# Sliding windows of an image batch: a plain unit filled and stored ahead of the second half-batch tile, in three pairs

## The chip, the core and the metric

The kernel runs on one core of a Trainium2 chip. The metric is the device time of one execution in microseconds, lower is better. Three engines matter: VectorE (DVE) and ScalarE (ACT) copy data within the on-chip memory SBUF, and GpSimd (POOL) issues indirect DMAs, whose destination rows come from an index tile. SyncE (SP) issues a few plain DMAs. The DMAs of all queues are carried out by the same 16 DMA engines.

## What is computed

The input x is 16 images of 64 channels of 64 x 64 f32 (16.8 MB). The output holds each 8 x 8 window with stride 4, that is 15 x 15 windows for each image (62.9 MB). Nothing is calculated; data is only moved.

```python
for i in range(n_h):
    for j in range(n_w):
        h_start = i * stride
        w_start = j * stride
        result[:, i, j] = x[:, :, h_start:h_start + window_size, w_start:w_start + window_size].copy()
```

One output row `(b, i, j)` is 64 x 8 x 8 f32 = 16 KB and contiguous.

## The kernel before

**Layout.** The whole input lies in one tile `L` of 128 partitions: a partition holds one half of the channels (`ch`, 2), one image (`b`, 16) and one quarter of the rows (`hq`, 4). The images are split into two half-batches of 8 (`y`, NY = 2), so that 32 partitions (`QP`) hold one half-batch and one channel half. A quarter of 16 rows has four window rows or slots (`s`); slots 0, 1 and 2 lie inside the quarter, slot 3 needs four rows of the next.

**Loads.** Eight DMAs on the queues of ACT and SP (line 115) bring the first channels through the buffers `GG` as a staging area, from where lines 125 to 132 copy them into `L`. Six DMAs on SP and 16 on POOL (line 58, called in lines 117 to 123) load the other channels straight into `L`, the half-batch y = 0 first and y = 1 behind it. POOL's loads and POOL's stores use the same queue.

**Buffers.** `GG` is four buffers of 128 partitions x 16 KB, one output row for each partition. `tile_()` (line 190) hands them out in turn, so a tile can be filled only when the store of the tile four places earlier has finished. There are 31 tiles.

**Three kinds of tile.**
- `part(y, j)` (line 195): one half-batch, slots 0 and 1, window columns j and j+1. It reads only the partitions of half-batch y. It takes 8 copies of 32 x 2048 f32, three on ACT and five on DVE, and one indirect store of 128 rows.
- `unit(j, 0, ...)`, a plain unit (line 212): all 16 images, slots 0 and 1, column j. It reads both half-batches. In the three pairs around the change it takes 4 copies of 64 x 2048, two on ACT and two on DVE, and one store of 128 rows.
- `unit(j, 2)`, a cross unit: slots 2 and 3. ACT copies; DVE fills its share with stream shuffles, which also fetch the rows of the next quarter. One store, of which 16 rows are dropped by the bounds check (112 are written).

`fill` (line 155) writes the copies of a unit; `scatter` (line 143) issues the store on POOL. Stores have no order among themselves, since each writes rows of its own.

**Order.** The program order in the source is the order on each engine. Tiles 0 to 2 are `part(0, 0)`, `part(0, 2)`, `part(0, 4)` (line 227). Then come three pairs (line 231), tiles 3 to 8: `part(1, 0)` and the plain unit of column 6, `part(1, 2)` and column 7, `part(1, 4)` and column 8. Behind them rounds of three cross units and one plain unit (line 234), tiles 9 to 28, and at the end two small tiles of column 14, which SP stores (lines 243 to 253).

Of the kernel before, what the change touches and what calls it, by code (L numbers as in the profile page):

```python
# [10 lines left out]
def kernel(  # L11
# [131 lines left out]
    def scatter(g, ix, j, s):  # L143
        st = nc.gpsimd.indirect_dma_start(  # L144
            out=o_v,
            out_offset=bass.IndirectOffsetOnAxis(ap=ix[:, 0:1], axis=0),
            in_=g.rearrange("p c r w -> p (c r w)"),
            in_offset=None,
            element_offset=(s * NW + j) * CFREE,
            bounds_check=B * NWIN - 1,  # L150
            oob_is_err=False,
        )
        free(st)

    def fill(g, half, s, j, lo, n, copies):

        d = slice(half * HP + lo, half * HP + lo + n)
        cols = slice(j * ST, j * ST + WS)
        for ch in (half, 1 - half):
            f = slice(ch * HP + lo, ch * HP + lo + n)  # L160
            cs = slice(ch * CL, (ch + 1) * CL)
            copy = copies[ch != half]
            if s < NSLOT - 1:
                copy(out=g[d, cs, :, :], in_=L[f, :, s * ST : s * ST + WS, cols])  # L164
            else:
                copy(out=g[d, cs, 0:ST, :], in_=L[f, :, s * ST : RB, cols])
                nc.vector.stream_shuffle(out=g[d, cs, ST:WS, :], in_=L[f, :, 0:ST, cols], mask=nxt)  # L167

    act, dve = nc.scalar.copy, nc.vector.tensor_copy
# [20 lines left out]
    def tile_():  # L190
        nonlocal at
        at += 1
        return G[(at - 1) % NG]

    def part(y, j):
        g = tile_()
        order = [(d, ch) for ch in range(CH) for d in range(P // QP)]
        for n, (d, ch) in enumerate(order):
            s, dj = d // NY, d % NY
            cols = slice((j + dj) * ST, (j + dj) * ST + WS)  # L200
            f = (ch * NY + y) * QP
            tc.keep_in_program_order(
                (act if n % 3 == 0 else dve)(  # L203
                    out=g[d * QP : (d + 1) * QP, ch * CL : (ch + 1) * CL, :, :],
                    in_=L[f : f + QP, :, s * ST : s * ST + WS, cols],
                )
            )
        scatter(g, (idx_y0, idx_y1)[y], j, 0)
# [3 lines left out]
    def unit(j, s, copies=(shf, mix)):  # L212
        nonlocal crossed
        g = tile_()
        if s == 0:
            fill(g, 0, 0, j, 0, HP, (act, copies[0]))
            fill(g, 1, 1, j, 0, HP, (act, copies[1]))
            scatter(g, idx, j, s)
        else:

            turn = 1 - crossed % 2
            crossed += 1
            fill(g, turn, s, j, 0, HP, (act, act))
            fill(g, 1 - turn, s + 1, j, 0, HP, (shf, mix))
            scatter(g, (idx_hi, idx_lo)[turn], j, s)
# [3 lines left out]
    plain = [(j, 0) for j in range(2 * EARLY, NW - 1)]  # L229
    cross = [(j, 2) for j in range(NW)]  # L230
    for n in range(EARLY):
        part(1, 2 * n)
        unit(*plain.pop(0), (dve, dve))
    while plain:
        for w in cross[:3]:
            unit(*w)
# [52 lines left out]
```

## Time and profile before

| | |
|---|---|
| median of three runs | 186.99 us (186.84 to 187.19) |
| the profiled execution | 187.06 us, span 185.3 us |
| DMA queue 0 (POOL: loads and stores) | 65.55 MB, 84.8% of 16 engines' span |
| DMA queue 1 (SP) | 8.13 MB, 11.0% |
| DMA queue 10 (ACT) | 2.10 MB, 3.1% |
| HBM read and written | 16.78 MB and 62.91 MB |
| L203 DVE COPY 32x2048 (half-batch tiles) | 30 of 1219 ns |
| L203 ACT COPY 32x2048 | 18 of 1897 ns |
| L164 ACT COPY 64x2048 (units) | 46 of 1897 ns |
| L164 DVE COPY 64x2048 | 6 of 1222 ns |
| L167 DVE STREAM_SHUFFLE 64x1024 | 30 of 1281 ns |

The span is the stretch that the profiler sees; some 1.8 us lie around it. Of the page's views, the tenths row shows how busy an engine, or the mean of the 16 DMA engines, was in each of 40 slices of 4.6 us. The timeline lists instructions by start and duration, equal neighbours merged ("x5"), with the idle time ahead of them and what ended it in brackets. The busy time by stretch can show a DMA share a little above 1, since packets overlap at their edges.

### The profile page before, as it was taken

The numbers are of one execution on the slowest core, as the hardware profiler recorded it, in microseconds if no ns is written. First come the engines' busy times: TensorE is split into PE (matmuls) and PEld (weight loads), VectorE is DVE, ScalarE is ACT, GpSimd is POOL, SyncE is SP. The second block draws the span as 40 slices with busy tenths as digits, with TensorE's granted clock in tenths as the row PEclk, the third lists the DMA queues.
The fourth block names the chain that finished last, engine by engine and source line by source line (L and its number), as shares of the span: only waits on it lengthen the run. The fifth ranks groups of instructions, "written<-read, shape, count | busy, mean of one in ns | idle before, by whom it ended". The sixth has DMA issues, their size and how long they took to land.

```text
span 185.3 us, 597 instructions
## 1 busy us (share of the span) xinstructions
DVE 154.2 (83%) x213; ACT 150.7 (81%) x100; POOL 48.3 (26%) x50
## 2 busy tenths in 40 slices
DVE  5002998999999999799999999999999999999600
ACT  0002999999999999998899999998999999899600
POOL 7400652033308071422222222222222222222000
DMA  4999999999999999999999999999999999999995
GB/s 151 398 410 399 402 402 399 390 382 426 433 424 435 428 428 439 432 430 424 435 430 432 428 432 428 439 417 435 424 423 428 410 435 414 421 428 403 442 414 216
DMA packets 10980, 75.81 MB, mean 409 GB/s; under 512 B 3280, under 2 KB 3280, under 8 KB 7376
## 3 DMA queue, kind: packets, MB, share of 16 engines
q0 software_dynamic: 8656, 65.55, 84.8%
q1 hardware_dynamic: 1744, 8.13, 11.0%
q10 hardware_dynamic: 576, 2.10, 3.1%
q14 instruction: 4, 0.03, 0.0%
HBM read 16.78 MB, written 62.91 MB: 430 GB/s over the span
## 4 chain that ended last, share of the span: by engine, by line
ACT 28%; DVE 28%; DMA 27%; issue 8%; POOL 2%; ACTq 1%; DVEq 0%; PEldq 0%
DVE GG L174 17%; ACT GG L203 17%; DMA L<-in_x_dram 14%; DMA out_dram<-GG,idx 13%; DVE GG L167 11%; ACT GG L164 7%; ACT GG L251 3%; POOL L L58 2%; ACT GG L178 1%; ACTq L284 0%; ACTq L203 0%; POOL pi L69 0%; DVEq L174 0%; PEldq L284 0%; ACTq L164 0%
## 5 line engine op out<-in xcount | busy, mean ns | idle before, releaser
L164 ACT COPY GG<-L 64x2048 f32<-64x2048 f32 x46 | 87.3, 1897 | 5.1 <-DMA out_dram<-GG,idx 2.7
L174 DVE STREAM_SHUFFLE GG<-L 64x1024 f32<-64x1024 f32 (+4 forms) x39 | 53.0, 1359 | 1.3
L167 DVE STREAM_SHUFFLE GG<-L 64x1024 f32<-64x1024 f32 x30 | 38.4, 1281 | 0.0
L203 DVE COPY GG<-L 32x2048 f32<-32x2048 f32 x30 | 36.6, 1219 | 1.8 <-DMA L<-in_x_dram 0.8
L203 ACT COPY GG<-L 32x2048 f32<-32x2048 f32 x18 | 34.1, 1897 | 0.7 <-DMA L<-in_x_dram 0.3
L132 DVE COPY L<-GG 32x2048 f32<-32x2048 f32 x10 | 11.9, 1234 | 13.7 <-DMA GG<-in_x_dram 13.6
L144 POOL DMA_INDIRECT out_dram<-GG,idx_y x6 | 11.0, 1838 | 26.3 <-DVE GG L203 13.2
L58 POOL DMA_DIRECT2D L<-in_x_dram x16 | 12.8, 809 | 19.0 <-DMA L<-in_x_dram 18.5
L144 POOL DMA_INDIRECT out_dram<-GG,idx_lo x8 | 7.7, 961 | 30.8 <-DVE GG L167 23.2
L132 ACT ACT_TABLE_LOAD x1 | 1.3, 1283 | 17.2 <-DMA GG<-in_x_dram 17.2
L144 POOL DMA_INDIRECT out_dram<-GG,idx x8 | 9.7, 1217 | 17.4 <-DVE GG L174 6.8
L144 POOL DMA_INDIRECT out_dram<-GG,idx_hi x7 | 6.7, 961 | 26.6 <-DVE GG L167 22.9
L132 ACT COPY L<-GG 32x2048 f32<-32x2048 f32 x6 | 11.2, 1894 | 0.1
L178 ACT COPY GG<-L 64x256 f32<-64x256 f32 (+2 forms) x21 | 10.2, 484 | 0.5
L164 DVE COPY GG<-L 64x2048 f32<-64x2048 f32 x6 | 7.3, 1222 | 0.2
L251 DVE COPY GG<-L 32x1280 f32<-32x1280 f32 x8 | 6.5, 818 | 0.4 <-DMA out_dram<-GG,idx_hi 0.3
L251 ACT COPY GG<-L 32x768 f32<-32x768 f32 x8 | 6.6, 829 | 0.1
L174 DVE LOAD_MASK_SELECT GG<-L x39 | 0.4, 9 | 1.4 <-ACT GG L164 1.0
L72 DVE TENSOR_SCALAR tb<-pi 128x1 int32<-128x1 int32 x1 | 0.2, 154 | 1.0 <-POOL pi L69 1.0
L179 DVE COPY GG<-L 64x1280 f32<-64x1280 f32 x1 | 0.9, 877 | 0.0
L78 DVE TENSOR_TENSOR th<-tc,tq 128x1 int32<-128x1 int32 x2 | 0.3, 156 | 0.0
L75 DVE TENSOR_SCALAR th<-tc 128x1 int32<-128x1 int32 x2 | 0.3, 154 | 0.0
(21 smaller groups left out, 3.0 us busy)
## 6 DMA issues: line engine op xcount, KB each, us to landing
L<-in_x_dram POOLq DMA_DIRECT2D x10, 768.0 KB, 18.4
L<-in_x_dram SPq DMA_DIRECT2D x6, 640.0 KB
GG<-in_x_dram ACTq DMA_DIRECT2D x4, 512.0 KB, 14.4
GG<-in_x_dram SPq DMA_DIRECT2D x4, 512.0 KB, 14.8
out_dram<-GG SPq DMA_DIRECT2D x2, 1024.0 KB, 10.1
L<-in_x_dram POOLq DMA_DIRECT2D x6, 128.0 KB, 18.2
out_dram<-GG,idx POOLq DMA_INDIRECT x8, 12.4
out_dram<-GG,idx_lo POOLq DMA_INDIRECT x8, 10.3
```

Of the source, the lines that this page charges most:

```text
L58: eng.dma_start(out=L[p0 : p0 + QP - HQ + 1 : HQ, c0:c1, :, :], in_=x_v[ch, y, q, :, c0:c1, :])
L75: nc.vector.tensor_scalar(out=d[:, :], in0=a[:, :], scalar1=float(m), scalar2=None, op0=ALU.mult)
L78: nc.vector.tensor_tensor(out=d[:, :], in0=a[:, :], in1=b[:, :], op=op)
L132: tc.keep_in_program_order(copy(out=L[d, c : c + PC, :, :], in_=S[ch][f, c : c + PC]))
L144: st = nc.gpsimd.indirect_dma_start(out=o_v, out_offset=bass.IndirectOffsetOnAxis(ap=ix[:, 0:1], axis=0), in_=g.rearrange("p c r w -> p (c ...
L164: copy(out=g[d, cs, :, :], in_=L[f, :, s * ST : s * ST + WS, cols])
L167: nc.vector.stream_shuffle(out=g[d, cs, ST:WS, :], in_=L[f, :, 0:ST, cols], mask=nxt)
L174: nc.vector.stream_shuffle(out=out, in_=in_, mask=same)
L178: act(out=out[:, 0:k], in_=in_[:, 0:k])
L179: other(out=out[:, k:], in_=in_[:, k:])
L203: (act if n % 3 == 0 else dve)(out=g[d * QP : (d + 1) * QP, ch * CL : (ch + 1) * CL, :, :], in_=L[f : f + QP, :, s * ST : s * ST + WS, cols],)
L251: copy(out=g[d, ch * CL + c0 : ch * CL + c1, :, :], in_=L[f, c0:c1, s * ST : s * ST + WS, cols])
```

## The change

Within each of the three pairs of line 231 the two tiles change places.

```diff
     plain = [(j, 0) for j in range(2 * EARLY, NW - 1)]
     cross = [(j, 2) for j in range(NW)]
     for n in range(EARLY):
+        unit(*plain.pop(0), (dve, dve))
         part(1, 2 * n)
-        unit(*plain.pop(0), (dve, dve))
     while plain:
```

The buffers go round as before, so the plain units now get tiles 3, 5 and 7 (buffers 3, 1, 3) and the half-batch tiles 4, 6 and 8 (buffers 0, 2, 0). On ACT two copies of a unit now stand ahead of three of a half-batch tile in each pair, on DVE two ahead of five, and on POOL the store with `idx` ahead of that with `idx_y1`. The number and the shapes of all instructions are the same. PE's and SP's streams are the same.

## The prediction

> **What bounds the kernel now.** I read the page's shares first, then the busy time by stretch, then the timeline between 44 and 90 us, then the list of waits, and last the trace's records of single DMA packets. Tiles are numbered 0 to 30 in the order in which the code takes a buffer; tile n lies in buffer n mod 4, and store n is its store.
>
> ```profile
> DVE 154.2 (83%) x213; ACT 150.7 (81%) x100; POOL 48.3 (26%) x50
> DMA  4999999999999999999999999999999999999995
> GB/s 151 398 410 399 402 402 399 390 382 426 433 424 435 428 428 439 432 430 424 435 430 432 428 432 428 439 417 435 424 423 428 410 435 414 421 428 403 442 414 216
> ```
>
> Both copy engines are over 80% busy, which looks like a bound. But the DMA row stands at 9 in every slice but the first and the last. By stretch (DVE, ACT and POOL busy, clock, DMA share, GB/s):
>
> ```profile
> 47.00:60.00 13.00, 12.66 (x12) 12.83 (x8) 5.50 (x3) 1.00 1.01 430
> 60.00:76.00 16.00, 14.62 (x12) 15.80 (x9) 5.82 (x4) 1.00 1.01 433
> 76.00:90.00 14.00, 13.44 (x24) 12.66 (x10) 2.89 (x3) 1.00 1.00 429
> 146.00:165.00 19.00, 18.73 (x31) 17.75 (x14) 3.85 (x4) 1.00 1.00 421
> ```
>
> All 16 DMA engines work all the time from the end of the loads on. The packet records say the same in single packets. Loads end at 46.8 us, the first store packet starts at 45.9, and there are 3600 store packets of 16 KB, 611 ns each at their quickest (also their median). 3600 x 0.611 / 16 = 137.5 us. Packets above 611 ns add 1.07 us in all. 45.9 + 137.5 + 1.1 = 184.5; the other 0.8 of the span of 185.3 is the stagger of the engines, which start and end a store up to a packet apart. So the DMA engines set the end, and an edit matters only if it gives them more bytes, slower packets, or a moment without a store to work on.
>
> The last is a matter of reserve: the time from the end of a store's issue on POOL to its first packet. These rows (start, duration) show the six tiles that the change touches:
>
> ```profile
> 53.08 3.82 ACT L164 COPY GG<-L 64x2048 f32<-64x2048 f32 x2
> 54.96 2.48 DVE L164 COPY GG<-L 64x2048 f32<-64x2048 f32 x2
> 55.70 1.86 POOL L144 DMA_INDIRECT out_dram<-GG,idx_y  x1 [4.40 <-ACT GG L164]
> 56.92 5.74 ACT L203 COPY GG<-L 32x2048 f32<-32x2048 f32 x3
> 57.47 6.23 DVE L203 COPY GG<-L 32x2048 f32<-32x2048 f32 x5
> 58.21 1.85 POOL L144 DMA_INDIRECT out_dram<-GG,idx  x1 [0.65 <-issue]
> 64.46 1.86 POOL L144 DMA_INDIRECT out_dram<-GG,idx_y  x1 [4.40 <-DVE GG L203]
> 66.42 6.22 DVE L203 COPY GG<-L 32x2048 f32<-32x2048 f32 x5 [0.22 <-DMA out_dram<-GG,idx_y]
> 66.97 2.04 POOL L144 DMA_INDIRECT out_dram<-GG,idx  x1 [0.65 <-ACT GG L164]
> 73.41 1.86 POOL L144 DMA_INDIRECT out_dram<-GG,idx_y  x1 [4.40 <-DVE GG L203]
> 76.14 0.01 DVE L174 LOAD_MASK_SELECT GG<-L  x1 [0.99 <-ACT GG L164]
> 76.39 0.97 POOL L144 DMA_INDIRECT out_dram<-GG,idx  x1 [1.12 <-ACT GG L164]
> ```
>
> Stores 3 to 8 are issued by 57.6, 60.1, 66.3, 69.0, 75.3 and 77.4. Counted off in the packet records (128 packets each), they begin at 60.8, 65.6, 70.5, 75.3, 80.2 and 85.1, so their reserves are 3.2, 5.5, 4.2, 6.3, 4.9 and 7.7 us. None is near zero. Later, DVE needs 18.6 us for three cross units and one plain unit (its first copies start at 90.67 and 109.27), while the DMA needs 17.7 (store 12 begins at 102.8, store 16 at 120.5). So the reserve shrinks: 7.4 at store 9, 6.0 at 12, 5.1 at 16, 4.0 at 24, and 3.4 at store 27 (issue at 165.71, 0.96 long; first packet at 170.1).
>
> **The change, part by part.** It removes and adds no instruction. In each of three pairs the tile of the second half-batch (8 copies of 32x2048) and the plain unit (4 of 64x2048) change places in the streams of ACT and DVE, and their two stores on POOL. SP's stream stays as it is. Both kinds of store have 128 packets, so the DMA's work is the same to the byte: 0 us. What moves is when each store is ready. I step through it on the rows above.
>
> Tile 3, now the plain unit. ACT is free at 47.31 (the chain has its next copy there), and takes 3.82: done at 51.1. DVE's last nine copies before 54.96 took 11.18 us, so the five of tile 3 began at 48.7; two copies take 2.48: done at 51.2. From DVE's end to the issue is 0.77 (54.93 to 55.70), so store 3 is issued at 52.0 instead of 55.7. This unit reads both half-batches, the displaced tile only the second; the second is the later to land, and the last load packet ended at 46.8, before either engine is free.
>
> Tile 4, now the half-batch tile, lies in the buffer of store 0, whose last packet ends at 51.6. A fill starts about 0.1 us behind that (tile 12's copy starts at 90.62, store 8 ended at 90.54). So it starts at 51.7, a wait that was not there: DVE stands idle 0.5 us. ACT to 57.4, DVE 51.7 + 6.2 = 57.9, issue at 58.7 instead of 58.2.
>
> Tile 5, the plain unit: ACT 57.4 to 61.3, issue at 62.0 instead of 64.5; DVE is done at 60.4. Tile 6 needs store 2, which ends at 61.34: DVE idles 1.05, works to 67.7, issue at 68.5 instead of 67.0. Tile 7: ACT to 71.0, issue at 71.8 instead of 73.4; DVE done at 70.2. Tile 8 needs store 4, which ends at 71.09: DVE idles 1.0, works to 77.4, issue at 78.2 instead of 76.4.
>
> The sum on DVE: idle time of 0.5 + 1.05 + 1.0 = 2.55 us takes the place of 0.22 + 0.99 (the rows at 66.42 and 76.14), so the first cross unit starts at 77.4 instead of 76.17, about 1.25 us late. The wait stands on DVE and ACT in program order; behind it is every later fill, and POOL's store waits for these. DVE has no slack after that, so I carry the 1.25 us to the end. Bounds for it: 0, if the landings are seen as early as the fills need them, and 2.55, if the idle of before is kept beside the new one.
>
> What hides it: the reserve. Stores 3 to 8 now have about 6.9, 5.1, 6.6, 5.0, 6.6 and 6.0 us (issue plus 1.86, or 0.96 for store 8, against first packets that don't move). The least of the whole run, at store 27, goes from 3.4 to 2.2 us; with the bound of 2.55 it is 0.9. The two last stores, on SP, go from 174.4 to about 175.6, and the packets of the second begin at 181.8. Without that cover the price would be the 1.25 us itself. Sum: 0 + 0 = 0 us, span 185.3. The profiled execution took 187.06 (span and 1.8 around it) and the median shown is 186.99, so I predict 187.0.
>
> A rule that speaks against moving stores: POOL's issue takes 1.76 to 2.04 us beside DVE's COPY and 0.96 beside its shuffles. The Trainium skill, page SBUF — State Buffer, section "SBUF: two separate sides", says why it may: a DVE copy in its two-port mode locks GpSimd out, which then can't write descriptors, and the DMA engines wait. The trace agrees with the slower issue, but not with waiting engines. By the page at its worst store 3 would be held until the five copies of tile 4 end.
>
> That case from rows: the copies end at 57.9, plus 1.86 is 59.8, and store 3's first packet is due at 60.8. It stays hidden.
>
> **The rivals.**
>
> A, forecast: the DMA has work throughout, and the end does not move: 187.0.
>
> B, slower: packets grow slower with a smaller reserve. Up to 116 us the packets cost 0.07 us more than at 611 ns, from 116 to 132 0.09, from 132 to 176 0.84, while the reserve falls from 7 to 3.4. If the reserve decides, below some 5 us, then 1.25 us less brings that point forward by one round of 18 us and raises the later rates: at 0.08 us per 4 us it costs 18 / 4 x 0.08 = 0.36, and a last round at 0.12 instead of 0.09 another 0.15 or more; about +0.6, or 187.6. For it: the two go together in time. Against it: stores 3 and 5 had reserves of 3.2 and 4.2 and packets of 611 ns. Address or phase can explain the rise as well.
>
> C, slower: the queue runs dry. It decides where DVE is more than 3.4 us late at store 27, its place; if the three waits add up instead of being absorbed (3 x 1.25 = 3.75), it costs 0.35, and each further wait its whole length: 187.4 to 188.6. Against it: each wait ends with a store whose time is fixed by the DMA, so lateness can't pile up within the three pairs.
>
> D, faster: the slow packets come in bursts of a dozen, once a store, 2.1 to 3.2 us behind its start, so they may hang on how the fills stand to the stores. Shifted by 1.25 us they may vanish: at most -1.07, half of it -0.5, or 186.5. Speaking for it is only the drift of the bursts.
>
> E: the change does not take effect, as the displaced tile was not late. Its effect on issue times follows from program order, but on time it is A: store 3's reserve of 3.2 was already enough, so the doubled reserve buys nothing.
>
> **How the numbers follow.** A and E together 0.64, B 0.16, C 0.08, D 0.12. What this kernel's measurement can tell from no change is about 0.2%, or 0.37 us; the runs of before lie within 186.84 and 187.19. B and C come out slower and D faster. Faster 0.13, within 0.2% 0.63, slower 0.24. The range: 186.5 takes in half of D, 187.6 takes in B and the near end of C.
>
> **What would show it.** Store 3 issued near 52, store 8 near 78 on POOL; new idle time on DVE of half a microsecond to one ahead of the three half-batch tiles, put down to a store; the first cross unit's shuffle near 77.4; POOL's last issues a microsecond later than 165.7 and 168.1; the DMA row still 9 throughout and 421 to 433 GB/s by stretch. A DMA share below 1.00 anywhere between 47 and 175 us, or GB/s that fall earlier than at 130, would make the prediction wrong.

## The result and the profile after

The changed kernel takes 186.56 us (median of 9 runs, 186.43 to 186.78) against 186.99 us (9 runs, 186.80 to 187.39): a ratio of 0.9974, with a 95% interval of 0.9964 to 0.9985. A second comparison, on another occasion, gave 186.50 against 186.87: 0.9980 (0.9971 to 0.9989). The kernel is faster by about 0.4 us, a quarter of a per cent, where no change was predicted.

The timeline of the changed kernel, in the rows that answer to those of before (start, duration, engine, line, operation; in brackets the idle time ahead and what ended it):

```profile
47.23 3.82 ACT L164 COPY GG<-L 64x2048 f32<-64x2048 f32 x2
48.65 2.47 DVE L164 COPY GG<-L 64x2048 f32<-64x2048 f32 x2
51.89 1.46 POOL L144 DMA_INDIRECT out_dram<-GG,idx  x1 [0.65 <-issue]
52.01 6.22 DVE L203 COPY GG<-L 32x2048 f32<-32x2048 f32 x5 [0.89 <-DMA out_dram<-GG,idx_y]
59.00 1.86 POOL L144 DMA_INDIRECT out_dram<-GG,idx_y  x1 [5.65 <-DVE GG L203]
61.49 6.22 DVE L203 COPY GG<-L 32x2048 f32<-32x2048 f32 x5 [0.76 <-DMA out_dram<-GG,idx_y]
61.85 2.24 POOL L144 DMA_INDIRECT out_dram<-GG,idx  x1 [0.99 <-ACT GG L164]
68.48 1.86 POOL L144 DMA_INDIRECT out_dram<-GG,idx_y  x1 [4.40 <-DVE GG L203]
71.16 6.22 DVE L203 COPY GG<-L 32x2048 f32<-32x2048 f32 x5 [0.94 <-DMA out_dram<-GG,idx_y]
77.42 1.27 DVE L174 STREAM_SHUFFLE GG<-L 64x1024 f32<-64x1024 f32 x1
78.15 0.97 POOL L144 DMA_INDIRECT out_dram<-GG,idx_y  x1 [4.40 <-DVE GG L203]
166.72 0.97 POOL L144 DMA_INDIRECT out_dram<-GG,idx_lo  x1 [3.77 <-ACT GG L164]
169.10 1.04 POOL L144 DMA_INDIRECT out_dram<-GG,idx  x1 [1.42 <-issue]
```

The three new waits of DVE are there (0.89, 0.76, 0.94), the first cross unit starts at 77.42 instead of 76.17, and POOL's last two issues come a microsecond later than before. All work behind tile 8 is later, and yet the kernel ends earlier. The tenths and the throughput of the page, and the stretches (DVE, ACT and POOL busy, clock, DMA share, GB/s):

```profile
DMA  5999999999999999999999999999999999999996
GB/s 158 394 409 402 397 400 403 390 381 428 427 433 429 433 433 426 433 438 426 433 427 429 436 426 433 429 429 436 427 426 426 426 426 418 426 422 383 443 408 262
```

```profile
146.00:165.00 19.00, 18.73 (x31) 18.06 (x14) 3.86 (x4) 1.00 1.00 422
165.00:175.00 10.00, 9.83 (x12) 8.99 (x10) 2.00 (x2) 1.00 0.99 416
175.00:184.80 9.80, 0.02 (x1) 0.00 (x0) 0.00 (x0) 1.00 0.80 341
```

At this grain nothing explains the gain; one stretch has even a DMA share of 0.99. The same last two stretches of before show where to look:

```profile
165.00:175.00 10.00, 8.83 (x10) 9.24 (x10) 1.99 (x2) 1.00 1.00 419
175.00:185.30 10.30, 0.00 (x0) 0.00 (x0) 0.00 (x0) 1.00 0.78 332
```

In the last one the DMA share is 0.78, and 0.80 after (part of the rest is the profiler's tail in both). Some engines of the 16 are done while others still work, so the packet records have to be taken apart.

First, their clock. The prediction set the end of the last packet equal to the end of the span, 185.28 us. On the clock of the timeline's rows the last packet of before ends at 184.03, its landing is signalled at 184.36, and the span goes on to 185.28. So every packet time of the prediction is 1.26 us late, and so is every "reserve" 1.26 us too large; lengths of packets and distances between packets are not touched. Packet times from here on are on the clock of the rows; the expectations quoted below still count reserves in the prediction's way.

A profiled span is, to within some 0.2 us, a sum of six terms: the start of the first store packet; 3600 x 0.611 / 16 = 137.5 us; the slow packets (all that packets took beyond 611 ns, divided by 16); the idle time of engines between 47 and 172 us (fewer than 16 packets in flight, as a mean over the 16 engines); the uneven end (the same from 172 us on, so how far the last engine ends behind the mean); and the tail of 1.26 us behind the last packet, which is the same to 0.02 us in these four profiles.

| profile | span | first packet | slow packets | idle 47-172 | uneven end |
|---|---|---|---|---|---|
| before | 185.28 | 44.62 | 1.07 | 0.03 | 0.76 |
| before, second profile | 185.15 | 44.65 | 0.94 | 0.04 | 0.75 |
| after | 184.82 | 44.53 | 0.69 | 0.42 | 0.28 |
| after, second profile | 184.69 | 44.52 | 0.66 | 0.33 | 0.34 |

Followed packet by packet to the end, before has 15 engines that end between 183.01 and 183.37, and one that ends at 184.03, about a packet (0.61 us) later. After has 10 engines between 183.38 and 183.55 and none behind them. By the means of the two profiles of each kernel, the uneven end is 0.45 us less and the slow packets 0.33 us less, and 0.34 us of new idle time is given back. A further 0.1 us is a first packet that came earlier, ahead of anything that the change touches. Idle time and uneven end together fall only from 0.79 to 0.69 us.

### The profile page after: what moved, and what is told of

Its sections match the earlier page's. It is cut to its first block, busy times and chain, and to the rows that moved or that the text cites. A ratio compares the mean times of both kernels' runs of the same rounds, so it can differ in the third digit from the quotient of the medians.

```text
span 184.8 us, 597 instructions
## 1 busy us (share of the span) xinstructions
DVE 154.3 (83%) x213; ACT 150.6 (82%) x100; POOL 49.8 (27%) x50
## 4 chain that ended last, share of the span: by engine, by line
DVE 53%; DMA 28%; issue 10%; POOL 2%; DVEq 1%; PEldq 0%
DVE GG L174 23%; DVE GG L167 16%; DMA out_dram<-GG,idx_y 15%; DMA L<-in_x_dram 14%; DVE GG L203 10%; DVE GG L251 3%; POOL L L58 2%; DVE GG L179 0%; DVEq L284 0%; DVE GG L164 0%; POOL pi L69 0%; DVEq L203 0%; PEldq L284 0%
## 5 line engine op out<-in xcount | busy, mean ns | idle before, releaser
L174 DVE STREAM_SHUFFLE GG<-L 64x1024 f32<-64x1024 f32 (+4 forms) x39 | 53.1, 1361 | 1.3
L167 DVE STREAM_SHUFFLE GG<-L 64x1024 f32<-64x1024 f32 x30 | 38.7, 1289 | 0.0
L58 POOL DMA_DIRECT2D L<-in_x_dram x16 | 13.9, 881 | 17.7 <-DMA L<-in_x_dram 17.2
L144 POOL DMA_INDIRECT out_dram<-GG,idx_y x6 | 10.1, 1690 | 27.6 <-DVE GG L203 18.8
L144 POOL DMA_INDIRECT out_dram<-GG,idx x8 | 10.9, 1360 | 17.5 <-DVE GG L174 9.9
L174 DVE LOAD_MASK_SELECT GG<-L x39 | 0.3, 9 | 0.0
```

The lines of the kernel that those rows point to most:

```text
L58: eng.dma_start(out=L[p0 : p0 + QP - HQ + 1 : HQ, c0:c1, :, :], in_=x_v[ch, y, q, :, c0:c1, :])
L144: st = nc.gpsimd.indirect_dma_start(out=o_v, out_offset=bass.IndirectOffsetOnAxis(ap=ix[:, 0:1], axis=0), in_=g.rearrange("p c r w -> p (c ...
L174: nc.vector.stream_shuffle(out=out, in_=in_, mask=same)
```

## Experiments

The first question was whether the gain comes from the order of the stores, or from the lateness that the change gives to all fills behind tile 8: 1.25 us at the first cross unit, and by POOL's issues (counted from its first store) still 0.9 to 1.1 us from tile 12 on. First, one pair alone:

```diff
-        part(1, 2 * n)
-        unit(*plain.pop(0), (dve, dve))
+        if n == 0:                     # last_pair: n == EARLY - 1
+            unit(*plain.pop(0), (dve, dve))
+        part(1, 2 * n)
+        if not (n == 0):
+            unit(*plain.pop(0), (dve, dve))
```

> Only the first of the three pairs changes places. Lateness theory (the gain comes from the fills of the rounds standing about 1.25 us later against the stores): by the step-through of the waits, DVE is back in step at tile 9 (first shuffle near 76.2, as before), so no gain: 186.9 to 187.1, slow-packet excess near 1.07 us. Order theory (the gain comes from which rows are stored next to each other): about a third of the 0.43 us, 186.8 to 186.9.

Measured: 186.88 against 186.88, ratio 0.9996 (0.9987 to 1.0005). DVE's first cross shuffle at 76.0, as worked out.

> Only the third pair changes places. Lateness theory: the half-batch tile 8 waits for store 4 (ends at 71.1), DVE starts tile 9 near 77.4, so the whole gain is there: 186.4 to 186.7, excess 0.6 to 0.8 us. Order theory: about a third of it, 186.8 to 186.9.

Measured: 186.71 against 186.88, 0.9989 (0.9980 to 0.9998); the cross shuffle at 77.64. The pair with the lateness has a gain, the one without has none.

Next, lateness without any change of order: work that is useless is added to the engine that is busiest.

```diff
             turn = 1 - crossed % 2
             crossed += 1
+            if crossed == 1:
+                dst = g[(1 - turn) * HP : (2 - turn) * HP, 0 : CL // 2, :, :]
+                src = L[(1 - turn) * HP : (2 - turn) * HP, 0 : CL // 2, 0:WS, 0:WS]
+                for _ in range(1):     # delay2: 2
+                    shf(dst, src)
             fill(g, turn, s, j, 0, HP, (act, act))
```

> The order of before, and one shuffle of the first cross unit (64x1024, 1.27 us on DVE) made twice. Lateness theory: extra work on a busy engine makes the kernel faster, 186.4 to 186.7, slow packets fewer from 116 us on. Order theory: nothing changes in the order of the stores, so 187.0. Reserve theory (rival B): 187.3 to 187.6.

Measured: 186.58 against 186.88, 0.9984 (0.9975 to 0.9993). Its profiled run was its slowest, 186.96. DVE's rows in tile 9 show the added shuffle (one of the two of L174 with 64x1024; four belong to the tile, and the two of L167 now stand last):

```profile
76.35 1.28 DVE L174 STREAM_SHUFFLE GG<-L 64x1024 f32<-64x1024 f32 x1
77.67 0.99 DVE L174 STREAM_SHUFFLE GG<-L 64x768 f32<-64x768 f32 x1
78.69 1.27 DVE L174 STREAM_SHUFFLE GG<-L 64x1024 f32<-64x1024 f32 x1
79.86 1.28 DVE L167 STREAM_SHUFFLE GG<-L 64x1024 f32<-64x1024 f32 x1
81.19 1.31 DVE L167 STREAM_SHUFFLE GG<-L 64x1024 f32<-64x1024 f32 x1
```

Lateness by itself makes the kernel faster, in the old order of stores. The reserve theory (rival B) falls, and a new order is not needed for a gain.

> The order of before, and one shuffle of the first cross unit made three times (2.5 us more on DVE). Lateness theory: at least the gain of one, 186.2 to 186.6, unless the reserve at store 27 (3.4 - 2.5 = 0.9 us) runs out. Order theory: 187.0. Reserve theory: 187.6 or more.

Measured: 187.83 against 186.88, 1.0049 (1.0035 to 1.0062). Twice the lateness costs a microsecond. Its stretches show a DMA share below 1, at full DVE load:

```profile
146.00:165.00 19.00, 18.72 (x30) 17.29 (x13) 3.85 (x4) 1.00 0.98 410
165.00:175.00 10.00, 9.82 (x14) 9.52 (x11) 2.00 (x2) 1.00 0.99 415
```

The time between the end of POOL's issue and the first packet, which I had called reserve, is 2.2 us at store 27 of before (3.4 in the prediction's count). Less the lateness of some 2.4 us it would be nothing, but it stops at 0.9 to 1.0 us, in stores 23, 26 and 27, while engines idle (1.1 us as a mean over the 16). That is a floor: the time that these stores need although engines stand without work. What the prediction could spend at store 27 of before is thus 2.2 - 1.0 = 1.2 us, and the change uses it up: 1.0 us is left there between issue and packet.

The next runs placed the lateness, with the same repeated shuffle at another cross unit (`crossed == 10`, tile 21), or took it back there by leaving a shuffle out:

```diff
-            fill(g, 1 - turn, s + 1, j, 0, HP, (shf, mix))
+            fill(g, 1 - turn, s + 1, j, 0, HP, (none if crossed == 10 else shf, mix))
```

> The order of before; the repeated shuffle stands in the first cross unit of the fourth round (tile 21, about 137 us), so DVE is 1.27 us late only from there to the end. Levelling theory (the gain is that the 16 DMA engines end together, because those that are ahead run out of packets near the end and the one that is behind catches up): the whole gain of the early repeat, 186.5 to 186.7, with no engine ending half a microsecond behind the others. Burst theory (the phase of the fills against the stores over the whole of the rounds decides how many packets are slow): a part of it, 186.7 to 186.8.

Measured: 186.68 against 186.87, 0.9991 (0.9982 to 1.0000); the engines end evenly (0.14 us).

> The shuffle repeated at tile 9, and one shuffle of tile 21 left out (a quarter of the fourth row block of one half stays as it was in the buffer, so 1024 elements of 64 partitions are not written), so DVE is 1.27 us late only from 77 to 137 us. Levelling theory: no gain, 186.8 to 187.0, and one engine ends a packet (0.6 us) behind the other 15, as in before. Burst theory: a part of the gain, 186.6 to 186.8, from fewer slow packets between 116 and 140 us.

Measured: 186.83 against 186.87, 1.0000 (0.9991 to 1.0009); uneven end 0.57 us, slow packets 1.12.

> The kernel before, for a second profile. Both theories: 186.9 to 187.0. Levelling theory: one DMA engine again ends about 0.6 us behind the rest; burst theory: the slow packets again add 0.9 to 1.1 us.

Measured: 186.93, ratio to before 1.0002 (0.9993 to 1.0011). This is what the comparison makes of no change. Its profile is in the table above.

> The changed kernel, for a second profile beside the others. Both theories: 186.4 to 186.7. Levelling theory: the last engines end within 0.2 us of each other; burst theory: the slow packets again add 0.6 to 0.8 us.

Measured: 186.50, as told above. The slow packets are again near 0.7 us. The last engine ends 0.17 us behind the packet that ended before it; in the second profile of before it is 0.58 us.

Up to here the levelling theory held: lateness at the end evens the engines. But the slow packets of `after` do not come from lateness: `delay1` (1.15) and `late_only` (1.07) have as many as before. So the order was tried without lateness: two pairs changed (`n < EARLY - 1`), and all three with one shuffle of tile 9 left out.

> The first two pairs change places, the third not; by the waits DVE is on time at tile 9 (near 76.1). Two-term theory (fewer slow packets come from the new order of stores 3 to 6; the even end of the 16 DMA engines comes from the lateness): slow-packet excess 0.65 to 0.85 us, but one engine again ends 0.5 to 0.7 us behind the mean, and the time is between, 186.7 to 186.9. Lateness theory alone: as before, excess 0.95 to 1.1, 186.85 to 187.0.

Measured: 186.85 against 186.90, 0.9998 (0.9989 to 1.0007). Slow packets 0.73, uneven end 0.93.

> The changed kernel with one shuffle of tile 9 left out (1024 elements of 64 partitions are not written), so that DVE is on time again from there on, as in before. Two-term theory: excess stays near 0.7 us, the last engine ends 0.7 us behind the mean again, no engine idles before 172 us; of the gain of 0.4 us about half is lost, 186.65 to 186.85. Lateness theory alone: all of it is lost, 186.85 to 187.0. Order theory alone: nothing is lost, 186.5.

Measured: 186.81 against 186.90, 0.9994 (0.9985 to 1.0003). Slow packets 0.57, uneven end 1.19 (its profiled run was its slowest, 187.14). The new order does lower the slow packets, but alone it gains nothing that can be told from no change, and the uneven end grows: in `two_pairs` 15 engines end between 182.64 and 183.00, some 0.4 us earlier than in before, and the last one at 183.80 (184.03 and 183.90 in the two profiles of before).

Two runs asked where the slow packets come from. `act`, or both kinds of shuffle, were made to do nothing in tiles 13 to 28:

```diff
+    def act(out, in_):
+        if not 13 < at < 30:
+            nc.scalar.copy(out=out, in_=in_)
```

> The order of before; ACT's copies of tiles 13 to 28 are left out (these stores write what the buffer held), DVE's shuffles stay and set the pace. If slow packets come from ACT's traffic in SBUF, the excess from 116 to 176 us (0.81 to 0.93 in before) falls under 0.3; if they come from the DMA and the HBM alone or from DVE, it stays. Time 186.3 to 187.0.

Measured: slow packets between 116 and 176 us 0.96 us (before: 0.94 and 0.82). The last packet ends at 183.98 us, as in before, but the span goes on for 2.42 us behind it instead of 1.26; so the time of 188.19, from a single run, says nothing of the stores.

> The order of before; DVE's shuffles of tiles 13 to 28 are left out (these rows keep what the buffer held), ACT's copies stay. ACT is quicker than the DMA, so the queue stays full and the stores are issued as soon as buffers come free. If slow packets come from DVE's traffic or from a queue that is nearly dry, the excess from 116 to 176 us falls under 0.3; if from ACT or the HBM it stays near 0.8. With a full queue no engine idles, so by the levelling theory one engine still ends behind the others.

Measured: slow packets 0.93 us, single run 186.70. Here the time from issue to first packet stood at 5.6 to 6.7 us from store 13 to 27. So slow packets do not hang on ACT's traffic alone or on DVE's alone, nor on a queue that is nearly empty; no run leaves out both. The Trainium skill, page SBUF — State Buffer, section "SBUF: two separate sides", says that a DMA can't be slowed by a compute operation; these two runs agree.

The last runs went after the place of the lateness and the new idle time. Repeats at tile 25 (`crossed == 13`):

> The order of before; one shuffle of tile 25 (the first cross unit of the last round, about 155 us) made twice, so DVE is 1.27 us late only over the last six tiles. Catch-up theory (lateness helps because the DMA engines that are ahead idle while the last one catches up, and this happens near the end): the gain of the earlier delays, 186.6 to 186.75, with the last engine less than 0.4 us behind the mean. If the lateness must act over a longer stretch (the rounds before 155 us): 186.8 to 186.9, the last engine 0.6 or more behind.

Measured: 186.89 against 186.94, 0.9998 (0.9989 to 1.0008). Uneven end 0.21, but idle 0.41. The end was evened and nothing gained: near the end, engines that wait and engines that end early are worth the same. The catch-up theory falls as I had put it.

> The same with the shuffle made three times, 2.5 us late over the last six tiles. By the floor of 2.2 us seen in the twofold delay at tile 9, the reserve there would be 1.2 us short at the end. Catch-up theory: the engines ahead idle about 1 us, the last one too; 187.0 to 187.5, and slower than the single repeat.

Measured: 188.12 against 186.94, 1.0065 (1.0051 to 1.0079), worse than expected. The first line is the stretch in which the queue runs dry:

```profile
146.00:165.00 19.00, 18.66 (x29) 17.82 (x14) 3.85 (x4) 1.00 0.95 398
165.00:175.00 10.00, 9.84 (x15) 9.03 (x10) 1.99 (x2) 1.00 0.97 406
```

Then the changed kernel with less lateness: ACT takes half of a shuffle's channels instead of a quarter (`split(CL // 2, shf)`), in the first two cross units or in the last round.

> The changed kernel; in the first two cross units (tiles 9 and 10) ACT takes 16 instead of 8 channels of the second half's share, so DVE's shuffle there is 64x512 instead of 64x768 (about 0.3 us less each): DVE is some 0.6 us late instead of 1.25. If lateness helps up to the point where the queue runs dry, and less is less: 186.6 to 186.75. If the idle time of 0.35 us near the end is pure loss: 186.3 to 186.5, better than the change.

Measured: 186.79 against 186.88, 0.9994 (0.9985 to 1.0003). By POOL's issues it is 0.7 us late at tile 10 and 0.3 us from tile 12 on, less than was planned. That keeps next to nothing; slow packets 0.57, uneven end 0.91.

> The changed kernel; the same larger share for ACT in the last round alone (tiles 25 to 27), so DVE is 1.25 us late up to 155 us and makes up about 0.9 us by tile 27. If the gain needs engines that idle near the end: most of it is lost, 186.7 to 186.9, the last engine over 0.5 us behind the mean. If the idle time there is pure loss: 186.2 to 186.45, with no idle time before 172 us.

Measured: 186.49 against 186.88, 0.9982 (0.9973 to 0.9991). Idle 0.10, uneven end 0.59, slow packets 0.62. DVE's shorter shuffle of the last round:

```profile
158.36 0.72 DVE L174 STREAM_SHUFFLE GG<-L 64x512 f32<-64x512 f32 x1
162.81 0.72 DVE L174 STREAM_SHUFFLE GG<-L 64x512 f32<-64x512 f32 x1
```

The gain stays though the lateness is taken back at the end and the idle time is nearly gone. Idle time and uneven end together are 0.69 us, as in the changed kernel: one went, the other came. So idle engines near 170 us are neither the means of the gain nor a loss on top of it. This version equals the change (0.9980 in its second comparison), it does not beat it.

Last, the order of before with the lateness from 137 to 155 us, and from 77 to 155 us:

> The order of before; the shuffle repeated at tile 21 and one shuffle of tile 25 left out (1024 elements of 64 partitions are not written), so DVE is 1.27 us late only from about 137 to 155 us. Window theory (what the kernels with a gain share, and the others lack, is a lateness of 1.25 us between 137 and 155 us): 186.6 to 186.75. Duration theory (the gain grows with the length of the lateness, and stretches of 20 to 60 us alone bring next to nothing): 186.8 to 186.95.

Measured: 186.78 against 186.88, 0.9993 (0.9984 to 1.0002), uneven end 0.49, idle 0.10.

> The order of before; the shuffle repeated at tile 9 and one shuffle of tile 25 left out, so DVE is late from 77 to 155 us, and on time at the end. Window theory: 186.55 to 186.75, as with the delay that lasts to the end (186.58). If the new order of the stores is needed for a gain without lateness at the end (as in the changed kernel that makes its lateness up): 186.8 to 187.0.

Measured: 186.66 against 186.88, 0.9991 (0.9982 to 1.0001), uneven end 0.35, idle 0.07. `mid_only` lies between what the theories expected, `to_155` in the range of the window theory, but neither interval excludes no change.

All medians side by side, as the difference to before on the same occasion:

| DVE late (us of the span) | order of before, or of the pairs named | all three pairs changed |
|---|---|---|
| never | +0.06 (before_again), 0.00 (first pair), -0.05 (two pairs) | -0.09 |
| less (0.7, then 0.3 us) from 77 | - | -0.09 |
| 77 to 137 | -0.04 | - |
| 137 to 155 | -0.10 | - |
| 155 to the end | -0.05 | - |
| 137 to the end | -0.19 | - |
| 77 to 155 | -0.22 | -0.39 |
| 77 to the end | -0.30 (delay1), -0.17 (last pair) | -0.43, -0.37 |

Each entry is uncertain by some 0.17 us, so no single row is much; those whose interval excludes no change are `delay1`, the last pair and the three near -0.4. The table agrees with the reading that lateness of about 1.2 us helps, more the longer it lasts, up to the point where the queue runs dry; but the rows between are too close to tell length from place. In the new order lateness helps by about 0.3 us (-0.09 to -0.4).

## Why the prediction was wrong

Right, and closely, was the whole step-through of the change. Store 3 was issued at 51.89 (predicted 52.0), store 8 at 78.15 (78.2); DVE's new idle time was 2.59 us (2.55); the first cross unit started at 77.42 (77.4); the store packets of tiles 3 to 8 did not move (59.52 and 83.83 for stores 3 and 8, 59.50 and 83.86 before); from issue to first packet at store 27 it lost 1.19 us (1.25). In part this was luck: the prediction let a fill start 0.1 us behind the last packet of the store that holds its buffer. The fills start 0.1 us behind the landing signal, which came 1.26 to 1.60 us behind the last packet of stores 0, 2 and 4; the packet clock, 1.26 us late, happened to hide that. Rival E's remark held too: the more than doubled reserve of store 3 bought nothing by itself, as the first pair alone shows.

Wrong was the last step, "Sum: 0 + 0 = 0 us". It rests on the DMA as one resource that is either busy or not, with a price per packet that a later fill does not touch. Two terms that the prediction had itself written down were taken as fixed: the 1.07 us of slow packets and the 0.8 us of "stagger of the engines". They are not fixed. The changed kernel's are 0.69 and 0.28, with 0.42 of idle time between. The stagger was also misread: 0.6 of the 0.76 us are one engine that ends a packet behind the other 15. The sign named for a wrong prediction did show, a DMA share of 0.99 from 165 to 175 us, but in a kernel that was faster.

Rival D named the right side and nearly the right time (186.5, which is also why the range took in 186.56), and one of the two causes: fewer slow packets, from fills that stand later against the stores. But its mechanism is not the one that runs: slow packets follow the new order of stores, not the lateness (`delay1` and `late_only` have as many as before, `two_pairs` and `after_ontime` have fewer without being late), and a shorter time shows only together with the lateness. So the nearness of its number is luck. At 0.12 its chance was too low: the prediction knew of 1.9 us of loss in the DMA that it could not explain, and held that an unexplained loss would stay where it is.

Rival B is refuted: the kernel with the smaller reserve had fewer slow packets, `delay1` at most 0.2 us more than before where B asked for 0.5, and `no_dve` with a full queue as many as before. Rival C was put at the wrong point: the reserve runs out not at 3.4 us of lateness but at 1.2. Of the 3.4 us, 1.26 are the packet clock, and 1.0 is the floor. So the bound of 2.55 us, which the prediction called hidden, would have cost: `delay2`, with that lateness, lost 0.95 us.

What is shown: lateness of the fills gains, in the old order and in the new; it goes with engines that end more evenly (an uneven end of 0.14 to 0.59 us in the eight profiles with the full lateness between 137 and 155 us, against 0.57 to 1.19 in the seven that are on time there or late by 0.3 us; `late_end`, late only behind that, has 0.21 and pays it in idle time); and the new order goes with fewer slow packets (0.57 to 0.73 us in six profiles with two or three pairs changed, 0.82 with the first pair alone, 0.94 to 1.15 in nine with neither; the last pair counts among the nine, and the kernels that run dry or leave out the copies of many tiles are in no group). The same groups part where the slow packets begin: between 116 and 132 us they add 0.01 us in all six, and 0.07 to 0.16 us in the nine. What stays open: why lateness evens the engines without making those ahead wait, as in `after_recover` and `to_155`; which engine ends last and why, as the trace does not number them (four 8 KB instruction packets, 0.31 us each, also run on them during the stores, and whether they fall on the last engine was not tested); and by what way the order of six stores near 70 us lowers the slow packets near 140 us. Single profiles vary by up to 0.4 us about the median of their kernel, so these terms can't be matched to the last tenth.

## What to carry to other kernels

When a group of parallel engines is busy to the last slice, the end is that of the last one of them, not of their mean: look at how evenly they end before calling a change to their supply free. A reserve in a queue must be counted from its floor, which is seen where the queue is driven dry (here 0.6 to 1.0 us), not from zero. Times of packets and of instructions must stand on one clock: a landing signal that seems to come ahead of its last packet says that they don't. And a loss that the profile shows but the prediction can't place (here 1.9 us of 185) is a chance of a gain or loss of that size, and belongs in the odds.

## What the runs showed of the hardware

- A store that engines were waiting for started 0.6 to 1.0 us behind the end of POOL's recorded issue (stores 23, 26 and 27 of `delay2`, 25 to 27 of `late_end2`). The Trainium skill, page DMA: Bandwidth & Descriptors, section "Specifications", gives about 1 us to the first byte on this path; measured from the end of the issue, these rows agree.
- In the kernel before, all but a few 16 KB store packets took 611 ns until about 116 us into the span; then bursts of slower ones came (mostly up to 0.1 us more), once or twice a store, with ACT's copies or with DVE's left out as with both. With two or three pairs changed the bursts began at about 132 us.
- One useless shuffle of 1.27 us on an engine that is 83% busy made the kernel 0.30 us faster (`delay1`).
